# Turning the keys without TensorE, joining four value products to other visits, and padding a bias tile, in a two-layer decoder kernel

## The chip, the core and the metric

The kernel runs on one core of one Trainium2 chip. The time is that of one execution on the device, in microseconds (us). The names of the engines are those of the profile: PE is TensorE (PEld its weight loads), DVE VectorE, ACT ScalarE, POOL GpSimd, SP the engine that only issues transfers.

## The reference, cut to what matters

Input x has 256 rows of 2048 numbers. Layer 1 is a Mamba-2 mixer, layer 2 a sliding-window attention mixer with shared keys and values; each ends in x <- LayerNorm(alpha * x + mixer(x)). All is float32.

```python
# layer 1, in short
z, xbc, dt_raw = split(x @ w_in)                       # 2048 -> 4096 + 6144 + 64
xbc = silu(causal_conv4(xbc));  dt = softplus(dt_raw + dt_bias)
y = ssd(xs, dt, -exp(a_log), B, C) + xs * d_skip       # chunks of 128, decays exp(cumsum(dt * a))
h = groupnorm(y * silu(z)) @ w_out
# before layer 2, once: 4 key heads and 4 value heads of 64
k, v = split(x @ kv_w + kv_b);  k = rope(k)            # first 16 of each 64 are turned
# layer 2: 32 query heads, window 128, one sink per head
q = rope(x @ wq + q_bias);  s = q k^T / 8 within the window
p = exp(s - m) / (sum exp(s - m) + exp(sink - m))
h = ((p v) * silu(x @ wg)) @ wb
```

## The kernel before

Every large product is made of three TensorE products, because each float32 operand is split in two parts: `wh` (rounded by ScalarE, line 164) and `wl` (the rest, by VectorE, line 167) for weights, `xH`/`xL`, `x1H`/`x1L`, `yH`/`yL`, `oH`/`oL` for the other operand. The products h*h, l*h and h*l are taken. A unit of weights is 128 x 2048 numbers; it lands as two halves in `wr` (6 buffers) and stands split in one of 4 buffers of `wh` and 4 of `wl`. A unit's two splits are written up to three units ahead of its products.

There are two shapes of large product. In the first (line 252, `mac`) the weights stand in the array and 256 columns of `xH`/`xL` or `x1H`/`x1L` move; a unit is 48 matmuls. It makes the input projections of both layers. In the second (lines 323 to 325, `out_unit`; line 1011, `x_stat`, for keys and values) the other operand stands in the array, `yH`/`yL`, `oH`/`oL` or `x1H`/`x1L`, and 512 columns of weights move; a unit is 12 matmuls for each half of the rows (h = 0 or 1). "OUT run" below is one such set of 12.

Everything else on TensorE is plain float32 and small, and is done in visits between two units: transposes against the identity, the scores (lines 1160 and 1167), the value products (line 1270 for h = 0; 1284 and 1291 for h = 1).

Layer 2 has four head groups j. The list `B_ORDER` fixes the order q0 g0 q1 g1 q2 o0 g2 q3 o1 g3 o2 o3, where q is a query block and g a gate block (4 units of the first shape each) and o an output block (4 weight units of the second shape, two OUT runs each). After each unit of q and g, and each weight unit of o, `tick()` counts down the list `pending`; `later(n, fn)` puts a piece of work n ticks ahead. So `later(3, ktr)` sets the transposes of the keys, `later(PV_AT[j][h], pv)` the value products, `MOVE_AT` the ScalarE copies that lay the probabilities out for them. `attend(j, 1)` comes three ticks after `attend(j, 0)`.

The keys leave the projection as rows (`kd`, 128 rows by 4 heads by 64, line 1060). GpSimd copies each head a second time beside itself (1066), TensorE turns four 128 x 128 pieces for each half of the rows (1071), and ScalarE copies them out of PSUM into `kT` (1074), where each head stands twice: on partitions 0 to 63 and on 64 to 127.

In layer 1, `sum_decay` (550) makes the exponents of the decays of four heads from `rb`, which a transfer brings back from memory, and `exp_decay` (557) exponentiates them. `plan` holds work that follows a block, `beside` work that is put inside `conv_silu` between its convolution and its tanh (line 497). ScalarE's instructions of `sum_decay` keep their order against all other pinned ones, so what stands behind them waits for them.

The tiles of layer 2 lie in the pool `bp` in the order in which their names are first used. `snk`, `rot`, `kT`, `vt`, the four `qT` and `kvb` share a start at multiples of 256 bytes; `qb` (line 1040) takes 64 bytes, and what follows it lies 64 bytes past a multiple of 256 in each partition:

| tile | start address before | past a multiple of 256 | after | past a multiple of 256 |
|---|---|---|---|---|
| oH, two buffers | 161600, 165696 | 64 | 161792, 165888 | 0 |
| oL, two buffers | 169792, 173888 | 64 | 169984, 174080 | 0 |
| pt0, ptw, pte (probabilities) | 119104, 123200, 157504 | 64 | 127488, 131584, 157696 | 0 |
| qT of odd j, two buffers | 127296, 129344 | 64 | 135680, 137728 | 0 |
| yH, yL, x1H, x1L, kT, vt, wh, wl | 106496, 114688, 179712, 196096, ... | 0 | the same | 0 |

(Addresses are those of the two built programs. All slices of oH, oL, yH, yL, x1H and x1L that stand in the array start at multiples of 512 bytes within their tile.)

Of the kernel before, what the change touches and what calls it, by code (L numbers as in the profile page):

```python
# [8 lines left out]
F32 = mybir.dt.float32  # L9
# [5 lines left out]
ALU = mybir.AluOpType  # L15
AX = mybir.AxisListType

P = 128
S = 256
# [42 lines left out]

MOVE_AT = [[2, 3, 3, 4], [3, 4, 5, 6]]
MOVE_LAST = [2, 3, 3, 4]
PV_AT = [[6, 7], [6, 7], [8, 7], [7, 5]]
RES_AT = [2, 2, 3, 3, 4, 5, 5, 6]
ALPHA = (2.0 * 2) ** 0.25
NEG = -1.0e30
# [15 lines left out]
def trunk(ctx: ExitStack, tc: tile.TileContext, A: dict, out: bass.AP, dbg=None):  # L84
    nc = tc.nc
    PSUM = bass.MemoryType.PSUM

    def pool(name, bufs=1, side=None, space=None, stack=ctx):
        kw = {"space": space} if space is not None else {}
        return stack.enter_context(  # L90
            tc.tile_pool(name=name, bufs=bufs, side=side, reuse_waits="tile", **kw)
        )
# [9 lines left out]
    def nm(s):  # L102
        uid[0] += 1
        return f"{s}_{uid[0]}"

    def mm_tile():
        return mm_ps.tile([P, 512], F32, tag="mm", name=nm("mm"), bufs=4)

    def ax_tile():
        return ax_ps.tile([P, 512], F32, tag="ax", name=nm("ax"), bufs=4)  # L110

    cc = cst.tile([P, 1024], F32, tag="cc", name="cc")
    ident = cc[:, 0:128]
# [131 lines left out]
    def next_unit(behind=False):  # L245
        load_next(min(used[0] + 1 + AHEAD, len(srcs)) - len(units), behind, not behind)
        used[0] += 1
        return units[used[0] - 1]
# [9 lines left out]
    def later(n, fn, place=None):  # L258
        pending.insert(len(pending) if place is None else place, [n, fn])
# [562 lines left out]
    beside = {}  # L822
# [6 lines left out]
    def at(t, fn, *a):  # L829
        plan.setdefault(t, []).append((fn, *a))  # L830
# [5 lines left out]
    for g in range(NG):  # L836
        t = 10 * g
        if g == 0:
            at(TD, turn_dt, *dts)
            at(4, load_decay, 0, 1)  # L840
            at(8, load_low, 0)
            pos = dict(cb=CB0, y=13)

            between[11] = [(turn_first, 0)]
            halves = [(5, 6, 7), (7, 8, 9)]
            by = (9, 10)
        elif g == 1:
            at(10, load_decay, 1, 0)
            at(10, load_decay, 1, 1)
            at(15, load_low, 1)  # L850
            pos = dict(cb=6, y=Y_AT, norm=10 + CB_AT)

            halves = [(13, 14, 15), (15, 16, 16)]
            by = (16, 17)
        else:
            at(t - 5, load_decay, g, 0)
            at(t - 5, load_decay, g, 1)
            at(t, load_low, g)
            pos = dict(cb=CB_AT, y=Y_AT, norm=10 + CB_AT)
        for hf in range(2):  # L860
            if g < 2:
                sa, sb, ex = halves[hf]
                if (g, hf) != (1, 0):
                    at(sa, sum_decay, g, hf, 0, 2)
                at(sb, sum_decay, g, hf, 2, 4)
                at(ex, exp_decay, g, hf)
            else:
                for i in range(2):
                    beside[t + 3 * hf + i] = sum_decay, g, hf, 2 * i, 2 * i + 2
                beside[t + 3 * hf + 2] = exp_decay, g, hf  # L870
        if g == 1:
            at(16, norm, 0)
        at(t + pos["cb"], cb, g)
        for hf in range(2):
            at(by[hf] if g < 2 else t + pos["cb"] + hf, by_cb, g, hf)
        if g > 0:
            xs_at = t + 6
            if g == 1:
                between[17] = [(turn_xs, 1)]
            else:  # L880
                at(xs_at, turn_xs, g)
            for n, js in enumerate(((0, 1), (2, 3))):
                at(xs_at + n + (g == 1), carry_xs, g, js)
            at(xs_at + 2, scale_xs, g)
        at(t + pos["y"], ymm, g)
        if g == 0:
            at(t + pos["y"], sum_decay, 1, 0, 0, 2)
        for i in range(4):
            at(t + pos["y"], gate, g, i)
        if g > 0:  # L890
            at(t + pos["norm"], norm, g)
# [36 lines left out]
    def center(h, mv, rs, nmr):  # L928

        for c in range(4):  # L930
            v = xr[:, h, c * 512 : (c + 1) * 512]
            if c % 2:
                nc.scalar.activation(v, v, AF.Identity, scale=rs[:], bias=nmr[:])
            else:
                nc.vector.tensor_scalar(v, v, mv[:, 0:1], rs[:], ALU.subtract, ALU.mult)
# [44 lines left out]
    bp = pool("bp")  # L980
# [8 lines left out]
    def rope(v, h, n):  # L989

        c = cs[:, h : h + 1, :].to_broadcast([P, n, 8])
        s = sn[:, h : h + 1, :].to_broadcast([P, n, 8])
        t = bp.tile([P, 4, 8, 8], F32, tag="rt", name=nm("rt"), bufs=1)
        x1, x2 = v[:, :, 0:8], v[:, :, 8:16]
        a, b, d, e = [t[:, i, :n, :] for i in range(4)]
        nc.vector.tensor_tensor(a, x1, c, ALU.mult)
        nc.vector.tensor_tensor(b, x2, s, ALU.mult)
        nc.vector.tensor_tensor(d, x2, c, ALU.mult)
        nc.vector.tensor_tensor(e, x1, s, ALU.mult)
        nc.vector.tensor_tensor(x1, a, b, ALU.subtract)  # L1000
        tc.keep_in_program_order(nc.vector.tensor_tensor(x2, d, e, ALU.add))

    def x_stat(ps, h, u, ui, pin=False, last=None):

        todo = [(k, i) for k in range(4) for i in range(3) if i != last]
        todo += [(k, last) for k in range(4) if last]
        for k, i in todo:
            kk = ui * 4 + k
            ks = slice(k * 512, (k + 1) * 512)
            hs = slice(h * P, (h + 1) * P)  # L1010
            m = nc.tensor.matmul(  # L1011
                ps[:], (x1H, x1L, x1H)[i][:, kk, hs], (u.h, u.h, u.l)[i][:, ks],
                start=(kk, i) == (0, 0), stop=ui == 3 and (k, i) == todo[-1],
            )
            pinned(m, pin)
# [20 lines left out]
    kT = bp.tile([P, 4, S], F32, tag="kT", name="kT")  # L1036
    vt = bp.tile([P, 2, S], F32, tag="vt", name="vt")
    kvb = bp.tile([P, 512], F32, tag="qT", name="kvb", bufs=2)
    nc.gpsimd.dma_start(kvb[:], A["kvb"].partition_broadcast(P))
    qb = bp.tile([P, 16], F32, tag="qb", name="qb")  # L1040
    nc.gpsimd.dma_start(qb[:], A["qb"])
    kv_u = []
    for h in range(2):
        ps = mm_tile()
        for ui in range(4):
            if h == 0:

                kv_u.append(next_unit(ui == 1))
                if ui == 0:
                    center(1, *scale1)  # L1050
            x_stat(ps, h, kv_u[ui], ui, h == 0, ((1, 1, 2, None), (1, None, None, None))[h][ui])
            if h == 0:
                for c in ((), (), (0, 1, 2, 3), ())[ui]:
                    if c % 2 == 0:
                        wide = bp.tile([P, 1024], F32, tag=("pt0", "pri")[c // 2], name=nm("x1"), bufs=1)
                    turn_x1(1, c, wide[:, c % 2 * 512 : c % 2 * 512 + 512])
                if ui == 3:
                    load_affine(0)
        kd = bp.tile([P, 4, 2, 64], F32, tag="qt", name=nm("kd"), bufs=2)
        nc.vector.tensor_tensor(  # L1060
            kd[:, :, 0, :], ps[:, :256].rearrange("p (j d) -> p j d", j=4),
            kvb[:, :256].rearrange("p (j d) -> p j d", j=4), ALU.add,
        )
        nc.vector.tensor_tensor(vt[:, h, :], ps[:, 256:], kvb[:, 256:], ALU.add)
        rope(kd[:, :, 0, :], h, 4)
        nc.gpsimd.tensor_copy(kd[:, :, 1, :], kd[:, :, 0, :])

        def ktr(h=h, kd=kd):
            pt = ax_tile()
            for j in range(4):  # L1070
                nc.tensor.transpose(
                    pt[:, j * P : (j + 1) * P], kd[:, j, :, :].rearrange("p a d -> p (a d)"), ident
                )
            nc.scalar.copy(kT[:, :, h * P : (h + 1) * P], pt[:].rearrange("p (j t) -> p j t", j=4))

        later(3, ktr)
    for c in range(1, 4):
        load_affine(c)
    for i, n in enumerate(RES_AT):
# [1 line left out]

    def rope_maps():

        nc.gpsimd.tensor_scalar(qb[:], qb[:], 0.125, None, ALU.mult)
        z = bp.tile([P, 2, 2, 32], F32, tag="rt", name="z", bufs=1)
        nc.vector.transpose(z[:].rearrange("p h m t -> p (h m t)"), turned[:].rearrange("p h m t -> p (h m t)"))
        for k in range(2):
            lo = 64 * k
            for a in range(4):
                nc.scalar.copy(  # L1090
                    rot[lo : lo + 32].rearrange("p m (h a t) -> p a m h t", h=2, a=4)[:, a],
                    z[32 * a : 32 * a + 32].rearrange("p h m t -> p m h t"),
                )
# [5 lines left out]
    sg = {}  # L1099
# [40 lines left out]
    def attend(j, h):  # L1140
# [161 lines left out]
        turn_far()  # L1302
        later(PV_AT[j][h], pv)
        if h == 0:
# [202 lines left out]
```

## Time and profile before

| what | us |
|---|---|
| three runs: median, lowest, highest | 982.09, 980.04, 982.14 |
| the profiled execution's own time | 980.68 |
| its span, first to last instruction | 978.6 |
| PE busy | 972.5 |
| DVE busy, ACT busy, POOL busy | 789.4, 666.5, 103.2 |

The span is 2.1 us shorter than the time of the same execution, which has a start and an end around it. The mean granted TensorE clock was 0.999 of full speed. A matmul's end is modelled, so how fast TensorE goes is read from the distance between two starts. Layer 1 fills the span up to about 657 us, the keys and values come to about 680, layer 2 to the end.

### The profile page before, as it was taken

How to read it: one execution, taken by the hardware profiler on the slowest of the kernel's cores; microseconds unless marked ns; L12 is line 12 of the kernel's file. 1: busy time of each engine (PE TensorE's matmuls, PEld its weight loads, DVE VectorE, ACT ScalarE, POOL GpSimd, SP SyncE). 2: the span in 40 equal slices, each digit the busy share in tenths (PEclk: the TensorE clock that was granted, in tenths of full speed). 3: DMA queues.
4: the chain of work that ended last, by engine and by line, in shares of the span. 5: the costliest groups of instructions: out<-in, count | busy, mean ns of one | idle time of the engine just before them, and what ended most of it. 6: DMA issues, size and time to landing. Idle time of an engine off the chain costs nothing.

```text
span 978.6 us, 18818 instructions
## 1 busy us (share of the span) xinstructions
PE 972.5 (99%) x7364; PEld 896.7 (92%) x7364; DVE 789.4 (81%) x1202; ACT 666.5 (68%) x1254; POOL 103.2 (11%) x145
## 2 busy tenths in 40 slices
PE   9999999999999999999999999999999999999997
PEld 8999989999999998999999999888999988988976
DVE  7888898976888877885887787889977778778786
ACT  7585885864985865776576487467567776784762
POOL 0000303004003001200300300412000000000003
PEclk9999999999999999999999999999999999999999
DMA  9788567755665766666666566458654645465632
GB/s 357 251 284 326 160 210 235 249 201 152 207 218 190 250 208 199 212 200 206 191 205 201 171 211 198 148 187 272 200 159 144 195 153 191 141 208 170 218 127 87
DMA packets 61274, 197.91 MB, mean 202 GB/s; under 512 B 6801, under 2 KB 11329, under 8 KB 60929
## 3 DMA queue, kind: packets, MB, share of 16 engines
q1 hardware_dynamic: 58528, 188.53, 58.5%
q0 software_dynamic: 2048, 7.65, 2.5%
q8 instruction: 58, 0.95, 0.4%
q10 hardware_dynamic: 608, 0.52, 0.2%
q14 instruction: 32, 0.25, 0.1%
HBM read 194.45 MB, written 2.23 MB: 201 GB/s over the span
## 4 chain that ended last, share of the span: by engine, by line
PE 90%; DVE 5%; ACT 2%; issue 1%; DMA 1%; DVEq 0%; ACTq 0%
PE mm L252 56%; PE mm L323 9%; PE mm L324 9%; PE mm L325 9%; PE mm L1011 2%; PE ax L654 2%; DVE wl L167 1%; ACT e L550 1%; DVE cv L494 1%; DMA rb<-rscr 1%; PE ax L1167 1%; DMA wr<-in_wa 1%; ACT wh L164 1%; PE ax L1160 0%; PE mm L390 0%
## 5 line engine op out<-in xcount | busy, mean ns | idle before, releaser
L167 DVE TENSOR_TENSOR wl<-wr,wh 128x1024 fp32r<-128x1024 f32 (+2 forms) x354 | 394.2, 1133 | 80.1 <-ACT wh L164 76.9
L164 ACT ACTIVATE wh<-wr 128x1024 fp32r<-128x1024 f32 (+2 forms) x354 | 333.3, 974 | 104.6 <-PE mm L252 65.9
L252 PE MATMUL mm<-xH,wh 128*128 128x256 f32 x1280 | 354.7, 277 | 0.1
L252 PE MATMUL mm<-xH,wl 128*128 128x256 f32 x1280 | 353.9, 276 | 0.0
L252 PE MATMUL mm<-xL,wh 128*128 128x256 f32 x1280 | 353.9, 276 | 0.0
L252 PEld LDWEIGHTS mm<-xH,wh 128*128 128x128 f32 x1280 | 240.4, 188 | 2.3 <-issue 0.9
L252 PEld LDWEIGHTS mm<-xL,wh 128*128 128x128 f32 x1280 | 240.4, 188 | 1.0
L252 PEld LDWEIGHTS mm<-xH,wl 128*128 128x128 f32 x1280 | 240.3, 188 | 0.0
L252 PE MATMUL mm<-x1H,wh 128*128 128x256 f32 x512 | 143.0, 279 | 0.0
L252 PE MATMUL mm<-x1L,wh 128*128 128x256 f32 x512 | 141.8, 277 | 0.0
L252 PE MATMUL mm<-x1H,wl 128*128 128x256 f32 x512 | 141.7, 277 | 0.0
L323 PE MATMUL mm<-wh,yH 128*128 128x512 f32 x256 | 101.3, 396 | 0.1
L324 PE MATMUL mm<-wh,yL 128*128 128x512 f32 x256 | 99.8, 390 | 0.0
L325 PE MATMUL mm<-wl,yH 128*128 128x512 f32 x256 | 99.7, 389 | 0.0
L252 PEld LDWEIGHTS mm<-x1H,wh 128*128 128x128 f32 x512 | 96.1, 188 | 3.9 <-issue 2.4
L252 PEld LDWEIGHTS mm<-x1L,wh 128*128 128x128 f32 x512 | 96.4, 188 | 0.1
L252 PEld LDWEIGHTS mm<-x1H,wl 128*128 128x128 f32 x512 | 96.2, 188 | 0.0
L670 POOL TENSOR_TENSOR yz<-yz,z 128x256 f32<-128x256 f32 x32 | 26.8, 848 | 451.9 <-DVE yz L665 451.9
L494 DVE SCALAR_TENSOR_TENSOR cv<-mm,pc,cv 128x255 f32<-128x255 f32 x144 | 68.7, 478 | 5.2 <-ACT cv L492 2.6
L323 PEld LDWEIGHTS mm<-wh,yH 128*128 128x128 f32 x256 | 48.1, 188 | 10.6 <-DVE z L584 1.1
L325 PEld LDWEIGHTS mm<-wl,yH 128*128 128x128 f32 x256 | 48.1, 188 | 10.1
L324 PEld LDWEIGHTS mm<-wh,yL 128*128 128x128 f32 x256 | 48.1, 188 | 9.1
(235 smaller groups left out, 1246.6 us busy)
## 6 DMA issues: line engine op xcount, KB each, us to landing
wr<-in_wa SPq DMA_DIRECT2D x154, 512.0 KB, 5.2
wr<-in_wo SPq DMA_DIRECT2D x64, 512.0 KB, 4.6
wr<-in_wq SPq DMA_DIRECT2D x32, 512.0 KB, 4.5
wr<-in_wg SPq DMA_DIRECT2D x31, 512.0 KB, 4.5
wr<-in_wb SPq DMA_DIRECT2D x16, 512.0 KB, 4.7
wr<-in_wb SPq DMA_DIRECT2D x32, 256.0 KB, 3.7
rb<-rscr SPq DMA_DIRECT2D x11, 512.0 KB, 6.0
wr<-in_wkv SPq DMA_DIRECT2D x8, 512.0 KB, 5.6
```

What stands on the lines that cost most here:

```text
L164: m = nc.scalar.activation(h[:, sl], v, AF.Copy)
L167: m = nc.vector.tensor_tensor(l[:, sl], v, h[:, sl].bitcast(F32), ALU.subtract)
L252: m = nc.tensor.matmul(ps, a, b, start=first and i == 0, stop=last and i == 2)
L323: pinned(nc.tensor.matmul(ps, aH[:, k, hs], u.h[:, ks], start=k == 0 and add is None, stop=False), pin)
L324: pinned(nc.tensor.matmul(ps, aL[:, k, hs], u.h[:, ks], start=False, stop=False), pin)
L325: pinned(nc.tensor.matmul(ps, aH[:, k, hs], u.l[:, ks], start=False, stop=k == 3), pin)
L494: nc.vector.scalar_tensor_tensor(a[:, sft:], ps[:, : S - sft], w(3 - sft), a[:, sft:], ALU.mult, ALU.add)
L550: m = nc.scalar.activation(e[:, h, cols], rb[:, h, c * P :], AF.Relu, scale=-1.0, bias=rtk[:, c, h0 + h : h0 + h + 1])
L654: nc.tensor.matmul(ps[64 * r : 64 * r + 64, cols], st.xd[:, c, i, 64 * r : 64 * r + 64], e[:, 256:] if c else e[:, :256], start=c == 0, st ...
L670: nc.gpsimd.tensor_tensor(v, v, st.z[i][:], ALU.mult)
L1011: m = nc.tensor.matmul(ps[:], (x1H, x1L, x1H)[i][:, kk, hs], (u.h, u.h, u.l)[i][:, ks], start=(kk, i) == (0, 0), stop=ui == 3 and (k, i) = ...
L1167: nc.tensor.matmul(pss[par][qs, at : at + 192], q2(rows, b + i, 64 * part, 64), kT[rows, j, 64 * part : 64 * part + 192], start=True, stop ...
```

## The change

Four things are changed.

The keys: `kd` is now 128 x 8 x 64 of which four heads are used, GpSimd's second copy and TensorE's transposes are gone. VectorE turns the 128 x 256 numbers of `kd` in 32 x 32 blocks into a new tile `zk`, once for each half of the rows, and 32 ScalarE copies carry the blocks to their place in `kT`, both copies of a head included. The copies run in four sets of eight, 3, 4, 7 and 8 ticks on. `zk` borrows one of the two buffers of the gate tile `sg`, which so gets its place in the pool earlier.

The value products of h = 0 (`pv`, first column of `PV_AT`) come 2 ticks later for j = 0, 1, 2 and one tick later for j = 3. The bias tile `qb` is padded to 256 bytes. The first half of `sum_decay(0, 0)` moves from behind block 5 into the convolution of block 6.

```diff
-PV_AT = [[6, 7], [6, 7], [8, 7], [7, 5]]
+PV_AT = [[8, 7], [8, 7], [10, 7], [8, 5]]
...
-                if (g, hf) != (1, 0):
+                if (g, hf) == (0, 0):
+                    beside[3] = sum_decay, 0, 0, 0, 2
+                elif (g, hf) != (1, 0):
                     at(sa, sum_decay, g, hf, 0, 2)
...
-    qb = bp.tile([P, 16], F32, tag="qb", name="qb")
-    nc.gpsimd.dma_start(qb[:], A["qb"])
+    qb = bp.tile([P, 64], F32, tag="qb", name="qb")[:, :16]
+    nc.gpsimd.dma_start(qb, A["qb"])
+    zk = bp.tile([P, 4, S], F32, tag="sg", name="zk", bufs=2)[:, :2].rearrange("p h (f t) -> p h f t", t=32)
...
-        kd = bp.tile([P, 4, 2, 64], F32, tag="qt", name=nm("kd"), bufs=2)
+        kd = bp.tile([P, 8, 64], F32, tag="qt", name=nm("kd"), bufs=2)[:, :4]
...
-        rope(kd[:, :, 0, :], h, 4)
-        nc.gpsimd.tensor_copy(kd[:, :, 1, :], kd[:, :, 0, :])
-
-        def ktr(h=h, kd=kd):
-            pt = ax_tile()
-            for j in range(4):
-                nc.tensor.transpose(
-                    pt[:, j * P : (j + 1) * P], kd[:, j, :, :].rearrange("p a d -> p (a d)"), ident
-                )
-            nc.scalar.copy(kT[:, :, h * P : (h + 1) * P], pt[:].rearrange("p (j t) -> p j t", j=4))
-
-        later(3, ktr)
+        rope(kd, h, 4)
+        nc.vector.transpose(zk[:, h].rearrange("p f t -> p (f t)"), kd.rearrange("p j d -> p (j d)"))
+
+        def carry_k(h, e):
+            for a in range(4):
+                for up in range(2):
+                    lo, at = 64 * up + 32 * e, h * P + 32 * a
+                    tc.keep_in_program_order(nc.scalar.copy(
+                        kT[lo : lo + 32, :, at : at + 32],
+                        zk[32 * a : 32 * a + 32, h].rearrange("p (j e) t -> p e j t", e=2)[:, e],
+                    ))
+
+        for e in range(2):
+            later(3 + e + 4 * h, lambda h=h, e=e: carry_k(h, e))
```

Three places show what moves. The first is ScalarE near 50 us, in layer 1: `e` holds the exponents of `sum_decay`, `ct`, `xs` and `cv` belong to the convolutions, `wh` to the weight splits. Before:

```order
L477 ACTIVATE f_441<-rtk 128x128
L550 ACTIVATE e_727<-rb_509,rtk 128x256
L550 ACTIVATE e_727<-rb_509,rtk 128x128
L550 ACTIVATE e_727<-rb_509,rtk 128x256
L499 ACTIVATE ct_643<-cv_644 128x256
L550 ACTIVATE e_727<-rb_509,rtk 128x128
L164 ACTIVATE wh_732<-wr_736 128x1024
L164 ACTIVATE wh_803<-wr_805 128x1024
L499 ACTIVATE xs_712<-cv_713 128x256
L492 ACTIVATE cv_792<-mm_742,pc 128x256
```

and after:

```order
L477 ACTIVATE f_441<-rtk 128x128
L164 ACTIVATE wh_727<-wr_731 128x1024
L499 ACTIVATE ct_643<-cv_644 128x256
L164 ACTIVATE wh_803<-wr_805 128x1024
L164 ACTIVATE wh_803<-wr_807 128x1024
L499 ACTIVATE xs_712<-cv_713 128x256
L492 ACTIVATE cv_787<-mm_737,pc 128x256
L550 ACTIVATE e_792<-rb_509,rtk 128x256
L550 ACTIVATE e_792<-rb_509,rtk 128x128
L550 ACTIVATE e_792<-rb_509,rtk 128x256
L550 ACTIVATE e_792<-rb_509,rtk 128x128
```

The four instructions that read `rb` now stand behind three weight splits and three steps of convolutions.

The second is ScalarE near 690 us, in the first query block; `qT` are the queries, and the two copies to `kT` of before go with the transposes on TensorE. Before:

```order
L164 ACTIVATE wh_8321<-wr_8323 128x896
L1074 COPY kT<-ax_8233 128x4x128
L1074 COPY kT<-ax_8239 128x4x128
L164 ACTIVATE wh_8321<-wr_8325 128x1024
L164 ACTIVATE wh_8388<-wr_8390 128x128
```

and after, the second of the four sets of eight:

```order
L164 ACTIVATE wh_8248<-wr_8250 128x768
L164 ACTIVATE wh_8248<-wr_8252 128x1024
L1075 COPY kT<-zk 32x4x32 x8
L164 ACTIVATE wh_8326<-wr_8328 128x128
L1121 ACTIVATE qT_8246<-mm_8185,qb 128x256
L164 ACTIVATE wh_8326<-wr_8328 128x896
```

The copies stand between the last split of one unit and the first of the next.

The third is TensorE near 940 us, the value products of j = 3 (`pt0`, `ptw`, `pte` are probabilities, `vt` the values). Before, the products of h = 0 stand 24 matmuls ahead of this piece, on their own between two OUT runs, and here are those of h = 1:

```order
L325 MATMUL mm_11080<-wl_10951,oH_10339 128x512
L1284 MATMUL ax_11095<-ptw,vt 64x256 x2
L1284 MATMUL ax_11096<-ptw,vt 64x256 x2
L1291 MATMUL ax_11095<-pte,vt 64x256
L1291 MATMUL ax_11096<-pte,vt 64x256
```

and after:

```order
L325 MATMUL mm_11092<-wl_10972,oH_10475 128x512
L1275 MATMUL ax_11109<-pt_8560,vt 64x512 x2
L1289 MATMUL ax_11116<-ptw,vt 64x256 x2
L1289 MATMUL ax_11117<-ptw,vt 64x256 x2
L1296 MATMUL ax_11116<-pte,vt 64x256
L1296 MATMUL ax_11117<-pte,vt 64x256
```

The products of h = 0 are now in one visit with those of h = 1. The same holds for j = 2; for j = 0 and j = 1 those of h = 0 join the scores of the next head group, `attend(j + 1, 0)`. All other rows of TensorE keep their order.

More of the change, by code (lines that the diff above doesn't have):

```diff
@@ L1058, in trunk @@
                     load_affine(0)
-        kd = bp.tile([P, 4, 2, 64], F32, tag="qt", name=nm("kd"), bufs=2)
+        kd = bp.tile([P, 8, 64], F32, tag="qt", name=nm("kd"), bufs=2)[:, :4]
         nc.vector.tensor_tensor(
-            kd[:, :, 0, :], ps[:, :256].rearrange("p (j d) -> p j d", j=4),
+            kd, ps[:, :256].rearrange("p (j d) -> p j d", j=4),
             kvb[:, :256].rearrange("p (j d) -> p j d", j=4), ALU.add,
@@ L1082, in rope_maps @@
     def rope_maps():
-        nc.gpsimd.tensor_scalar(qb[:], qb[:], 0.125, None, ALU.mult)
+        nc.gpsimd.tensor_scalar(qb, qb, 0.125, None, ALU.mult)
         z = bp.tile([P, 2, 2, 32], F32, tag="rt", name="z", bufs=1)
```

## The prediction

> **What bounds the kernel now.** I read the table of busy times first, then the waits of TensorE, then stretches of TensorE's timeline around each place that the change touches, and last the rows of ScalarE and VectorE at those places.
>
> ```profile
> PE 972.5 (99%) x7364; PEld 896.7 (92%) x7364; DVE 789.4 (81%) x1202; ACT 666.5 (68%) x1254; POOL 103.2 (11%) x145
> ```
>
> TensorE is busy for 972.5 of 978.6 us of span, and the view of its waits has a single entry, 1.0 us at the very start. So time is won only by fewer matmuls, by matmuls that follow each other faster, or by closing small seams between groups. What the other engines gain or lose counts only if TensorE comes to wait for it. Since the end of a matmul is modelled, I take its pace from the distance between two starts.
>
> ```profile
> 696.07 0.28 PE L252 MATMUL mm<-x1H,wl 128*128 128x256 f32 x1
> 696.18 1.04 PE L1071 MATMUL ax<-cc,kd 128*128 128x128 f32 x8
> 696.97 0.36 PE L252 MATMUL mm<-x1H,wh 128*128 128x256 f32 x1
> 697.17 0.28 PE L252 MATMUL mm<-x1L,wh 128*128 128x256 f32 x1
> ```
>
> ```profile
> 804.50 0.40 PE L325 MATMUL mm<-wl,oH 128*128 128x512 f32 x1
> 804.83 1.08 PE L1270 MATMUL ax<-pt,vt 128*64 128x512 f32 x4
> 805.83 0.50 PE L323 MATMUL mm<-wh,oH 128*128 128x512 f32 x1
> 806.17 0.39 PE L324 MATMUL mm<-wh,oL 128*128 128x512 f32 x1
> ```
>
> These are, on TensorE's timeline, two visits of small float32 matmuls: the eight key transposes, and the value products of j = 0, h = 0. Steady starts are 0.11 us apart at line 252 and 0.23 in an OUT run; around a visit one gap ahead and one behind are longer.
>
> **Key transposes taken off TensorE.** From 696.18 to 696.97 they hold it 0.79 us. The first matmul behind them takes 0.20 to the next start instead of 0.11. Removing both gives 0.79 + 0.09 = 0.88 us.
>
> **Four visits merged into others.** The products stay, their seams go. Entry: 804.50 to 804.83 is 0.33 instead of 0.23. Exit: 805.83 to 806.17 is 0.34 instead of 0.23. So a seam costs 0.10 + 0.10, and four of them 0.80 us. The merged products are all float32 like the visit that they join, so I add nothing for the joint.
>
> **The padded tile.** It moves `oH` and `oL` from 64 bytes past a multiple of 256 to a multiple. They are the operand that stands in the array in an OUT run. Here are 24 matmuls of such runs, first with `yH`, which lies on a multiple, then with `oH`:
>
> ```profile
> 640.91 0.39 PE L323 MATMUL mm<-wh,yH 128*128 128x512 f32 x1
> ...
> 646.35 0.39 PE L323 MATMUL mm<-wh,yH 128*128 128x512 f32 x1
> ```
>
> ```profile
> 808.73 0.40 PE L323 MATMUL mm<-wh,oH 128*128 128x512 f32 x1
> ...
> 814.33 0.40 PE L323 MATMUL mm<-wh,oH 128*128 128x512 f32 x1
> ```
>
> With `yH` 24 starts take 5.44 us, 226.7 ns each; with `oH` 5.60, 233.3 each. The shapes and types are the same; the runs of line 1011, whose `x1H` lies on a multiple too, go like `yH`. Lines 323 to 325 have 124 matmuls of 512 columns each on `oH` or `oL`: 372 x 6.7 ns = 2.5 us, and 24 of 256 columns at some 4 ns 0.1. If the address makes the difference, 2.6 us go; if not, nothing. No row shows `oH` at another address, but the runs differ in nothing else that I can find, so I take the whole 2.6 and keep 0 as the other end.
>
> The Trainium skill, "TensorE: Matmul & The Clock Gate", in the part "Step-by-step: what each phase is for", says that the array has two read ports of its own and that loading the next tile's weights takes no bandwidth from the running matmul. By that the place of the standing operand could not change the pace and this term would be 0; the 226.7 and 233.3 speak against it, though they can't say which property of `oH` does it.
>
> The probabilities `pt0`, `ptw`, `pte` and the `qT` of odd j move likewise, but their matmuls are plain float32, and the scores of odd and even j show no difference of pace. Nothing for these. There is one slow unit that I can't explain, just behind a value visit:
>
> ```profile
> 780.61 0.39 PE L252 MATMUL mm<-x1H,wh 128*128 128x256 f32 x1
> ...
> 786.25 0.28 PE L252 MATMUL mm<-x1H,wl 128*128 128x256 f32 x1
> ```
>
> 47 gaps take 5.64 us, 120 ns each, where the first rows above have 0.11. Four units, two behind each h = 1 value visit of j = 0 and 1, lose about 0.2 each this way. If the alignment of `pte` and `ptw` cured them, 0.8 would come on top; the merged visits might as well slow more units. I take 0, and price both among the rivals.
>
> **The decay sums.** The view of waits has this for ScalarE, and TensorE's timeline that at the end of the first stretch that hangs on it:
>
> ```profile
> ACT e L550 <- DMA rb<-rscr: 2.6, 1, 2.6
> ```
>
> ```profile
> 129.82 0.28 PE L252 MATMUL mm<-xH,wl 128*128 128x256 f32 x1
> 130.17 0.50 PE L323 MATMUL mm<-wh,yH 128*128 128x512 f32 x1
> ...
> 135.51 0.39 PE L325 MATMUL mm<-wl,yH 128*128 128x512 f32 x1
> 136.02 0.36 PE L252 MATMUL mm<-xH,wh 128*128 128x256 f32 x1
> ```
>
> The chain of work that ended last runs through the return of `rb` at 42 to 49, these sums, and the transfer of weights below, up to the matmul at 130.17.
>
> ```profile
> 52.99 5.06 DMA wr<-in_wa
> ```
>
> After the change three splits and three convolution steps stand ahead of the sums, so the 2.6 us of waiting go to work that was behind it. But TensorE, up to there, waits little: 0.35 instead of 0.11 at 130.17, and 0.51 instead of 0.23 at 136.02, 0.52 in all. The gain lies between 0 (the weight transfer of 5.06 is late next) and 0.52; I take the middle, rounded to 0.3.
>
> **What VectorE, ScalarE and GpSimd get instead.** No row of before has the new copies; the nearest are equal in size, the turned rotation map and the block turns of layer 1:
>
> ```profile
> L625 DVE STREAM_TRANSPOSE zx<-xs 128x256 f32<-128x256 f32 x28 | 12.0, 438 | 0.9
> ...
> L1090 ACT COPY rot<-z 32x128 f32<-32x128 f32 x8 | 2.4, 296 | 1.4 <-DVE z L1086 1.3
> ```
>
> ```profile
> 690.86 0.42 ACT L164 ACTIVATE wh<-wr 128x256 fp32r<-128x256 f32 x1 [2.69 <-issue]
> ...
> 713.51 0.31 ACT L164 ACTIVATE wh<-wr 128x128 fp32r<-128x128 f32 x1 [1.67 <-PE mm L252]
> ```
>
> 32 copies x 0.296 = 9.5 us on ScalarE, in four bursts of 2.4; two turns x 0.438 = 0.9 us on VectorE; GpSimd loses two copies and ScalarE two. I cost it all at nothing, and the cover is this. Each burst falls into the place between two units' splits, where ScalarE idles 1.7 to 3 us (the bracketed 2.69 and 1.67). The tightest is 0.7 over, and a unit's splits stand up to three units, some 16 us, ahead of its matmuls. If that lead were gone, the full 9.5 us would show. Behind a burst wait the query rows (`qT`) and VectorE's `wl` splits, which have the same lead. The keys themselves are needed here:
>
> ```profile
> 718.97 1.16 PE L1160 MATMUL ax<-kT,qT 64*128 64x128 f32 x16
> ...
> 736.64 1.53 PE L1167 MATMUL ax<-kT,qT 64*64 64x192 f32 x32
> ```
>
> The bursts go at ticks 3, 4, 7 and 8; a tick is one unit of 5.5 us, and the old `ktr` at tick 3 stood at 696. So the first half is there by about 704, the second by about 726, a burst included: 15 and 10 us early. `zk` borrows a buffer of `sg`, whose next use is in the first gate block, where the copies already are or soon will be done; a wait there would fall on ScalarE and DVE, with the same lead behind it. No queue of transfers is passed: the change issues the same transfers, `qb` from GpSimd's queue included.
>
> **The later value products.** For j = 0, 1, 2 they still lie well ahead of their output block. For j = 3 this is not so: products, gate, `oH`, `oL` and the OUT run follow closely.
>
> ```profile
> 941.39 0.50 PE L323 MATMUL mm<-wh,oH 128*128 128x512 f32 x1
> ```
>
> ```profile
> 945.02 0.75 DVE L1258 TENSOR_TENSOR o<-ax,sg 128x256 f32<-128x256 f32 x2
> ...
> 946.82 0.69 DVE L1299 TENSOR_TENSOR oL<-o,oH 128x512 fp32r<-128x512 f32 x1
> ```
>
> Here h = 1 of before takes from the end of the visit at 941.39 to 947.51 until `oL` is there, 6.1 us. After the change h = 0 comes out of that same visit, and its first OUT run is 24 matmuls, some 5.5 us, behind it. At VectorE's old pace that would be 0.6 late; but h = 0 is first in VectorE's and ScalarE's new order and need not stand behind the `xr` adds that took part of the 6.1. I take 0 and keep up to 2.5 as a rival.
>
> **Sum.** 0.88 + 0.80 + 2.6 + 0.3 = 4.58, say 4.6 us. The profiled execution's own time is 980.68, so 976.1; it stands 1.4 under the median of 982.09, from which the same sum gives 977.5. I take the middle of the two, a base of 981.4, and so **976.8**.
>
> **The rivals.** All go from the base of 981.4.
>
> The pad does nothing: the slow pace belongs to `oH` for another cause. Then 2.0 is left, 979.4. For it: no row shows one tile at two addresses. Against it: three aligned operands go at one pace, the unaligned one at another.
>
> The four slow units turn fast as well: 4.6 + 0.8 = 5.4, 976.0. For it: `pte` and `ptw` are the operands of just those visits. Against it: the units behind them don't read these tiles.
>
> `oH` of j = 3 comes late and TensorE waits 2.5: 979.3. It decides when products to `oL` take over 5.5 us; the 6.1 above speaks for it, the order on VectorE against it.
>
> More units fall into the slow pace behind the merged visits: up to 12 x 0.2 = 2.4 back, 979.2.
>
> Slower: ScalarE's copies are not hidden. Place: from 690 to 730. All of 9.5 less 4.6, 4.9 slower, **986.3**. It decides when a burst exceeds ScalarE's idle time and the splits have no lead, or when a copy that moves between partitions takes several times 0.296. For it: ScalarE is 68% busy and its idle slots are no longer than a burst. Against it: the lead of three units. The Trainium skill, "VectorE: DVE Perf Modes", in "The three transpose paths", has it that VectorE turns 32 x 32 blocks only, and that 128 x 128 goes through TensorE where PSUM will do as the target; it speaks for the way of before, and no run so far shows what the blocks cost here.
>
> **How the numbers follow.** Chances: the sum as it stands 0.52, with the four units 0.14, pad without effect 0.16, `oH` late 0.06, more slow units 0.05, copies not hidden 0.07. About 0.2%, 1.96 us, can be told from no change, so faster means under 980.1. The first two cases are faster; the three around 979.3 lie 0.8 from the bound, and with runs that scatter by 2 us half of each, 0.13, counts as faster, the rest as the same. That makes 0.79 faster. The last case gives 0.07 slower, and 0.14 is left for the same. Low end: all terms at their best (0.52 for the sums, 0.8 for the units, the pad's 2.6), 5.6 off the lowest run of 980.04, 974.4. High end: the pad without effect from the median, 980.1, and some scatter, 980.5. Only the copies not hidden and a few ends of the others lie outside, under 2 in 10.
>
> **What the profile after would show.** No line 1071, and the unit at about 696 following its neighbour without a seam. OUT runs on `oH` at 227 ns; 233 would be the failure of the largest term. One visit fewer at four places. The wait of ScalarE for `rb` gone. 32 rows of copies near 0.3 us, no wait of TensorE for `wh`, `wl` or `kT` between 690 and 740, and none for `oH` or `oL` near 946. I would be wrong above all by the cause of the 233 ns, next by a copy far above 0.3 us.

## The result and the profile after

| | before | after |
|---|---|---|
| median of 10 runs, us | 981.47 (979.32 to 983.62) | 977.32 (976.65 to 979.88) |
| profiled execution, own time and span | 980.68, 978.6 | 977.57, 975.7 |

The ratio is 0.9964, 95% interval 0.9955 to 0.9972: 3.5 us faster, 2.7 to 4.4. The forecast was 976.8. The page of the changed kernel and the view of TensorE's waits:

```profile
PE 969.3 (99%) x7356; PEld 896.6 (92%) x7356; DVE 788.8 (81%) x1204; ACT 675.0 (69%) x1284; POOL 100.4 (10%) x143
```

```profile
PE ax L372 <- DVE zero L360: 1.0, 1, 1.0
PE mm L323 <- DVE xr L330: 0.6, 1, 0.6
PE mm L324 <- DVE oL L1304: 0.3, 1, 0.3
```

The two lower waits are new. Where the transposes stood, TensorE's timeline now runs through at its steady 0.11:

```profile
696.09 0.28 PE L252 MATMUL mm<-x1H,wl 128*128 128x256 f32 x1
696.20 0.28 PE L252 MATMUL mm<-x1H,wh 128*128 128x256 f32 x1
```

Two rows of the OUT runs, 24 matmuls apart, 5.44 us, 226.7 ns each:

```profile
950.56 0.39 PE L323 MATMUL mm<-wh,oH 128*128 128x512 f32 x1
...
956.00 0.39 PE L323 MATMUL mm<-wh,oH 128*128 128x512 f32 x1
```

The new groups cost what their neighbours in size did, and a burst fills the place in front of a unit's first split on ScalarE:

```profile
L1075 ACT COPY kT<-zk 32x128 f32<-32x128 f32 x32 | 9.5, 296 | 0.4
...
L1069 DVE STREAM_TRANSPOSE zk<-kd 128x256 f32<-128x256 f32 x2 | 0.9, 435 | 0.0
```

```profile
710.90 2.44 ACT L1075 COPY kT<-zk 32x128 f32<-32x128 f32 x8
713.36 0.31 ACT L164 ACTIVATE wh<-wr 128x128 fp32r<-128x128 f32 x1
```

The new wait near 809 stands in TensorE's timeline between two OUT runs, and the row of VectorE behind it is an add on `xr`, which frees the accumulator that the run wants:

```profile
808.74 0.39 PE L325 MATMUL mm<-wl,oH 128*128 128x512 f32 x1
809.74 0.50 PE L323 MATMUL mm<-wh,oH 128*128 128x512 f32 x1 [0.61 <-DVE xr L330]
```

```profile
809.01 0.67 DVE L330 SCALAR_TENSOR_TENSOR xr<-xr,mm 128x512 f32<-128x512 f32 x1
```

That the add ends at 809.68 and the matmul starts at 809.74 shows the tie. Before, the same add ended at 809.57 and the run that needs its accumulator started 1.96 later:

```profile
808.90 0.67 DVE L330 SCALAR_TENSOR_TENSOR xr<-xr,mm 128x512 f32<-128x512 f32 x1
```

```profile
811.53 0.40 PE L323 MATMUL mm<-wh,oH 128*128 128x512 f32 x1
```

The one near 945 is for `oL` of j = 3, h = 0:

```profile
944.53 0.39 PE L323 MATMUL mm<-wh,oH 128*128 128x512 f32 x1
945.21 0.50 PE L324 MATMUL mm<-wh,oL 128*128 128x512 f32 x1 [0.29 <-DVE oL L1304]
```

```profile
944.48 0.68 DVE L1304 TENSOR_TENSOR oL<-o,oH 128x512 fp32r<-128x512 f32 x1
```

Cutting the executions at fixed matmuls tells more than one total. Each number is the distance between two starts on TensorE, the last the span less the start of the last matmul. "After, again" is a second profiled execution of the changed kernel (below).

| stretch, us | before | after | after, again |
|---|---|---|---|
| first steady unit starts at | 23.59 | 24.44 | 23.79 |
| from there to the unit at about 150 | 126.38 | 125.60 | 125.60 |
| from there to the end of keys and values (680) | 529.85 | 529.80 | 531.41 |
| layer 2: from there to the last matmul | 293.34 | 290.83 | 290.86 |
| the end, behind the last matmul | 5.42 | 5.00 | 5.00 |

Layer 2 repeats within 0.03 us, layer 1 varies by more than a microsecond between executions of one program. So layer 2 is where parts of the change can be weighed from one trace, and its 2.51 splits like this (the term of the OUT runs is the one that the pad alone shows, below; the others are sums over the runs and visits in the two traces): transposes and their seam 0.87 less; 31 OUT runs on `oH` 2.12 less; the slow unit of line 252 at 838 turned normal, 0.18 less; joined visits about 1.2 less; against these three waits, 0.94 near 809, 0.59 near 945, and 0.31 in the visit of the scores at 836, which took 1.77 instead of 1.46.

### The profile page after: what moved, and what is told of

The parts are those of the page before. It is cut to its first block, busy times and chain, and to the rows that moved or that the text cites. A ratio compares the mean times of both kernels' runs of the same rounds, so it can differ in the third digit from the quotient of the medians.

```text
span 975.7 us, 18826 instructions
## 1 busy us (share of the span) xinstructions
PE 969.3 (99%) x7356; PEld 896.6 (92%) x7356; DVE 788.8 (81%) x1204; ACT 675.0 (69%) x1284; POOL 100.4 (10%) x143
## 4 chain that ended last, share of the span: by engine, by line
PE 93%; DVE 3%; ACT 2%; issue 1%; DVEq 0%; ACTq 0%
PE mm L252 61%; PE mm L323 8%; PE mm L324 8%; PE mm L325 8%; PE ax L654 2%; PE mm L1013 2%; DVE wl L167 1%; ACT wh L164 1%; PE ax L1172 0%; PE ax L1165 0%; PE ax L591 0%; PE mm L390 0%; ACT p L1200 0%; ACT ptw L1233 0%; DVE z L1214 0%
```

## The experiments

**The pad alone.**

```diff
-    qb = bp.tile([P, 16], F32, tag="qb", name="qb")
+    qb = bp.tile([P, 64], F32, tag="qb", name="qb")[:, :16]
```

> The kernel before with the bias tile padded to 256 bytes and nothing else; the order of instructions is that of before. If the address of the standing operand makes the pace: starts in the OUT runs on oH and oL go from 233 to 227 ns, 31 runs x 0.08 = 2.4 us less, so about 979.1 where before has 981.5. If that pace belongs to oH for another cause, or the gain in the changed kernel came from the merged visits: 233 ns stay and the time is the same within 0.5 us. The slow units of line 252 behind the value visits at 780 and 831 should stay slow (118 to 120 ns), since pte and ptw at a multiple of 256 did not cure them in the changed kernel; if they go, alignment plays a part there after all.

Measured: 980.25 beside 981.04, ratio 0.9989 (0.9977 to 1.0001). The pace changed as the address has it; 24 matmuls take 5.44 us:

```profile
951.39 0.39 PE L323 MATMUL mm<-wh,oH 128*128 128x512 f32 x1
...
956.83 0.39 PE L323 MATMUL mm<-wh,oH 128*128 128x512 f32 x1
```

The 31 full runs went from 87.93 to 85.81 us. Of these 2.12, layer 2 kept 1.58 (291.75): the visit of the scores at 837 grew by 0.49, and the unit at 697 went at the slow pace, 0.20. So the address sets the pace of these runs, and a part of the gain is taken back by other waits. In the whole time 2.4 less was expected, and the interval allows anything from 2.3 less to nothing: the trace shows the gain, the median alone does not.

**The opposite sign, and the moving operand.** `yH` and `yL` moved to 64 past a multiple of 256; in another kernel `x1H` and `x1L` to 192 past (their pool is laid from the right-hand end, so 64 bytes more for `x1L` move both down).

```diff
-                yp.tile([P, 4, S], F32R, tag="yH", name=nm("yH"), bufs=2),
+                yp.tile([P, 4 * S + 64], F32R, tag="yH", name=nm("yH"), bufs=2)[:, 16 : 16 + 4 * S].rearrange("p (k s) -> p k s", s=S),
...
-    x1L = x1s.tile([P, KT, S], F32R, tag="x1L", name="x1L")
+    x1L = x1s.tile([P, KT * S + 16], F32R, tag="x1L", name="x1L")[:, : KT * S].rearrange("p (k s) -> p k s", s=S)
```

> The kernel before with yH and yL of layer 1 put 64 bytes past a multiple of 256, where oH and oL lie; the order of instructions is that of before. This is the opposite sign of the pad on twice as many runs. If the address of the standing operand makes the pace: the 64 OUT runs of layer 1 go from 2.72 to 2.80 us, 64 x 0.08 = 5.1 us more, about 986.6. If it is anything else about oH: no change, 981.5 within 0.7.

> The kernel before with x1H and x1L put 192 bytes past a multiple of 256 (64 short of the next); the order of instructions is that of before. The two stand in the array in the 96 matmuls of line 1011, and move through it in 1536 matmuls of line 252. If only the standing operand's address counts: line 1011 goes from 227 to 233 ns, 96 x 6.7 ns = 0.6 us more, 982.1, and line 252 stays at 114 ns. If the moving operand's address counts as well, by the same 3% of its pace: 1536 x 3.4 ns = 5.2 us on top, about 987. If neither: 981.5.

Measured: 984.67 (ratio 1.0039, 1.0025 to 1.0052, so 3.8 us more) and 988.55 (1.0078, 1.0064 to 1.0091, 7.7 more). Of `yH`, 24 matmuls took 5.60 us:

```profile
641.46 0.39 PE L323 MATMUL mm<-wh,yH 128*128 128x512 f32 x1
...
647.06 0.39 PE L323 MATMUL mm<-wh,yH 128*128 128x512 f32 x1
```

From 150 us on 56 runs of layer 1 went from 154.02 to 157.80, 0.07 each where 0.08 was expected. With `x1H` moved, one steady unit of line 252 (48 matmuls, both rows being the first of a unit) takes 5.69 us, where before has 5.45:

```profile
748.58 0.28 PE L252 MATMUL mm<-x1H,wh 128*128 128x256 f32 x1
...
754.27 0.28 PE L252 MATMUL mm<-x1H,wh 128*128 128x256 f32 x1
```

```profile
743.66 0.28 PE L252 MATMUL mm<-x1H,wh 128*128 128x256 f32 x1
...
749.11 0.28 PE L252 MATMUL mm<-x1H,wh 128*128 128x256 f32 x1
```

Layer 2 grew by 7.03. Line 1011, where `x1H` stands in the array, grew only by 0.22 in 96 matmuls, 2.3 ns each, not the 6.7 that I had expected. So the address of the moving operand counts as well, by 4.6 ns per matmul where I had reckoned with 3.4.

**Other offsets: 96 and 128 bytes past a multiple of 256.** The same edit as the pad, with 24 and 32 columns.

> The kernel before with the bias tile at 96 bytes, which puts oH and oL 96 bytes past a multiple of 256. A slice of 128 columns is 512 bytes in a partition. If what counts is a multiple of 256 or of 128: starts in OUT runs stay at 233 ns. If a multiple of 32 were enough, 64 past would have been fast as well, so 227 is not expected from any theory; a pace above 233 would say that it depends on more than aligned or not.

> The kernel before with the bias tile at 128 bytes, which puts oH and oL 128 bytes past a multiple of 256; with 96 past, the OUT runs went at 233 ns as with 64. If a multiple of 128 is enough: 227 ns. If it takes a multiple of 256: 233 ns.

Measured in one execution each, 981.65 and 983.11, so that only the pace can be read. 24 matmuls take 5.62 us with 96, and 5.57 with 128:

```profile
950.65 0.40 PE L323 MATMUL mm<-wh,oH 128*128 128x512 f32 x1
...
956.27 0.39 PE L323 MATMUL mm<-wh,oH 128*128 128x512 f32 x1
```

```profile
949.09 0.39 PE L323 MATMUL mm<-wh,oH 128*128 128x512 f32 x1
...
954.66 0.40 PE L323 MATMUL mm<-wh,oH 128*128 128x512 f32 x1
```

A multiple of 128 is not enough for `oH` and `oL`; of the offsets tried (0, 64, 96, 128) only 0 is fast in these runs of 512 columns.

It does not follow that the operand in the array must start at a multiple of 256. In line 252 of layer 2 this operand is `wh` and `wl`, whose slices the source places by hand (`BROKEN`): of the 16 slices of a unit the first starts 0 bytes into `wh` and 7872 into `wl`, 192 past a multiple of 256, and the fifteen others start at 576 and 64 bytes, 64 past. The moving `x1H` and `x1L` lie at a multiple. A steady unit of before, its first, third and last matmul:

```profile
743.66 0.28 PE L252 MATMUL mm<-x1H,wh 128*128 128x256 f32 x1
...
743.90 0.28 PE L252 MATMUL mm<-x1H,wl 128*128 128x256 f32 x1
...
749.00 0.28 PE L252 MATMUL mm<-x1H,wl 128*128 128x256 f32 x1
```

The first two gaps, at the slice with 0 and 192, take 0.24 us, 120 ns each; the 45 others take 5.10, 113.3 each. So 64 past is the fast place here. The unit at 707.96, in which the source lays the second slice at 0 and 192 too (`BROKEN2`), has the two gaps of 120 ns at its second slice as well, before and after. And the 24 matmuls of 256 columns on `oH` and `oL` did not gain by the pad: 11 gaps take 1.30 us before and 1.31 to 1.32 after. What sets the pace is therefore not the place of one operand alone; the place of the other and the number of columns come in. The rule behind it stays open.

**The keys, the value products and the decay sums, each alone** on the kernel before (the diff of the change, its part).

> The kernel before with only the keys turned by VectorE and carried by 32 ScalarE copies; no pad, value products and decay sums as before. If the copies are hidden: TensorE's visit of 0.79 and its seam of 0.08 go, 0.87 us, about 980.6 where before has 981.5. If they are not hidden, up to 9.5 us come on top, so anything above 982.

> The kernel before with only the value products of h = 0 put later. Theory: four seams go, 0.8 us; but without the visit at 805 TensorE catches up with VectorE's adds on xr and waits there about 0.8 to 1.0, as in the changed kernel near 809, and for oL of j = 3 about 0.5 to 0.7 near 945. The OUT runs on oH are at 233 ns here, 0.08 slower each, which gives VectorE up to 0.3 us back before 809. So between 0.3 less and 0.6 more than before, 981.2 to 982.1: the joining alone wins nothing. Rival: the two waits come from the faster OUT runs of the pad; then they are not there, and 980.5.

> The kernel before with only the first half of sum_decay(0, 0) moved. By the comparison of the two traces TensorE loses its stalls near 130 and 136: 0.8 us less, 980.7. If the weight transfer were late next, as the prediction allowed: nothing, 981.5.

| kernel | median, us | ratio, interval | layer 2, us | end, us |
|---|---|---|---|---|
| keys | 979.95 | 0.9982 (0.9973 to 0.9991) | 292.42 | 5.00 |
| value products | 981.02 | 0.9990 (0.9980 to 1.0000) | 292.59 | 5.85 |
| decay sums | 981.86 | 0.9999 (0.9988 to 1.0010) | 293.34 | 5.79 |
| pad (above) | 980.25 | 0.9989 (0.9977 to 1.0001) | 291.75 | 5.86 |

The kernel before, run beside the first three, had a median of 982.05. In layer 2 (293.34 before) the keys win 0.92, the value products 0.75, the pad 1.58, together 3.25; the whole change has 2.51. What is missing is put down to waits that only the faster TensorE meets: 1.84 us of them in the whole change, more than in any part alone. The keys won more in the medians than the 0.87 that was expected: 1.8, with an interval from 0.9 up, and their end is 0.42 shorter than that of before. The value products alone met the wait for `xr` already (0.2 in the view of waits), at the old pace of the OUT runs, but not the one for `oL`, which was expected too.

The decay sums win nothing that can be measured, though they do what was expected of them near 130:

```profile
130.35 0.28 PE L252 MATMUL mm<-xH,wl 128*128 128x256 f32 x1
130.46 0.39 PE L323 MATMUL mm<-wh,yH 128*128 128x512 f32 x1
```

0.11 where before has 0.35. From the first steady unit to 150 the six profiled executions with moved sums all take 125.60. Of the eight without, two with `yH` or `x1H` moved left aside, 125.60 twice, and 126.38, 126.65, 127.10 and 128.24. But in four of the six the gain is given back at 261 to 270, where TensorE waits for a convolution step; the first execution of the changed kernel and that of the decay sums alone show no such wait. In the second execution of the changed kernel:

```profile
269.60 0.28 PE L252 MATMUL mm<-xH,wl 128*128 128x256 f32 x1
270.52 0.36 PE L252 MATMUL mm<-xH,wh 128*128 128x256 f32 x1 [0.64 <-DVE cv L494]
```

The mean time at which the fourth visit of line 654 starts (302 to 305 us) is 303.2 for the six with moved sums and 303.0 for the six without. What makes VectorE late at 270 stays open.

**Two bursts instead of four.**

```diff
-            later(3 + e + 4 * h, lambda h=h, e=e: carry_k(h, e))
+            later(4 + 4 * h, lambda h=h, e=e: carry_k(h, e))
```

> The changed kernel with the four sets of eight copies made into two sets of sixteen, at ticks 4 and 8: ScalarE is taken for 4.7 us in one piece, more than the 1.7 to 3 us that it idles between two units' splits. If the lead of the splits (up to three units, 16 us) is the cover: no change from the changed kernel, 977.3 within 0.5, and no wait of TensorE for wh or wl. If the cover is only the idle time: 2 x (4.7 - 3) = 3.4 us more, about 980.7.

Measured: 979.38, ratio 0.9980 (0.9971 to 0.9989), and layer 2 at 292.51, 1.68 more than the changed kernel. Neither theory has it. Between 690 and 740 each unit and visit takes the same as in the changed kernel within 0.01. But ScalarE does not recover. The first row is a burst on its timeline, the second `oH` of j = 0; in the changed kernel (third row) the same `oH` stands 3.02 earlier, of which TensorE's own offset at that time explains 1.38:

```profile
694.63 4.91 ACT L1075 COPY kT<-zk 32x128 f32<-32x128 f32 x16
...
772.89 0.63 ACT L1303 ACTIVATE oH<-o 128x512 fp32r<-128x512 f32 x1 [0.22 <-DVE o L1263]
```

```profile
769.87 0.63 ACT L1303 ACTIVATE oH<-o 128x512 fp32r<-128x512 f32 x1 [0.21 <-DVE o L1263]
```

Apart from the bursts, ScalarE's and VectorE's orders are the same in both. The 1.6 us are carried along for 90 us, until the scores at 787 wait for an accumulator that `o` still holds:

```profile
786.76 0.88 PE L1172 MATMUL ax<-kT,qT 64*64 64x192 f32 x16
788.56 1.21 PE L1172 MATMUL ax<-kT,qT 64*64 64x192 f32 x16 [0.92 <-DVE o L1263]
```

So the lead of the splits hides a burst from the next units, and does not pay for it.

**The changed kernel again, and with value products put back.**

```diff
-PV_AT = [[8, 7], [8, 7], [10, 7], [8, 5]]
+PV_AT = [[8, 7], [6, 7], [10, 7], [8, 5]]
...
+PV_AT = [[8, 7], [6, 7], [10, 7], [7, 5]]
```

> The changed kernel once more, beside the next two on the same chip. If its two new waits belong to the order of its instructions: TensorE again waits for xr near 809 (0.6 by the view of waits) and for oL near 945 (0.3), and the time is 977.3 where before has 981.5. If they were chance in one execution: they are absent or elsewhere.

> The changed kernel with the value products of j = 1, h = 0 back at 6 ticks, so that they stand on their own between two OUT runs near 804 again. If the joined visit took away the pause in which VectorE caught up with its adds on xr: the wait near 809 goes, 1.0 us with its seams, and one seam of 0.2 returns, 0.8 us less than the changed kernel, 976.5. If VectorE is late there for another reason: the wait stays and the kernel is 0.2 slower, 977.5.

> As the one above, and the products of j = 3, h = 0 back at 7 ticks. The wait for oL near 945 cost 0.6 to 0.7 us with its seam; a joined visit is worth 0.35 there. If that wait comes from the later products, another 0.3 us less, 976.2; if it comes from the faster OUT runs, it stays and the kernel is 0.35 slower than the one above. So no more than 0.3 either way: this is the best version that I can see from the two traces.

Measured beside one kernel before at 981.48: 977.59 (0.9956, 0.9942 to 0.9970), 978.48 (0.9967, 0.9954 to 0.9980), 979.56 (0.9971, 0.9960 to 0.9982). Layer 2: 290.86, 291.49, 291.31. The two new waits came back in the second execution at the same places, 0.6 and 0.3, so they belong to the program. The last line of the diff is the third kernel. With j = 1 put back the wait for `xr` went, 0.94 us with its seams, and this took its place (view of waits):

```profile
PE ax L1172 <- DVE o L1263: 1.2, 1, 1.2
```

The visit at 836 grew by 1.42. With j = 3 put back as well, `oL` was waited for no more; as the later products alone did not meet this wait either, it takes both them and the faster runs. Neither version beats the changed kernel, though the waits went that were to go, and 976.5 and 976.2 were expected in that case: the waits are shifted from one place to the next, since VectorE's chain of softmax, `o` and `xr` runs hardly earlier when TensorE does (its add on `xr` started at 809.01 after and 808.90 before, while TensorE had won 1.08).

## Why the prediction was right

The time lay in the range, 0.5 from the forecast. The terms were not as near as that; errors of both signs cancelled.

- Key transposes, 0.88 forecast: 0.87 in the trace, 0.92 in layer 2 of the keys alone. Right.
- Four seams, 0.80: about 1.2. The seam was sized rightly to 0.03; I added nothing for the joint, but the products themselves are shorter behind or ahead of other small products (line 1270: 1.01 before, 0.91 for j = 2 and 3). The visit at 804.83 is that of j = 1, not of j = 0 as the prediction has it; its rows and their sum are right.
- The padded tile, 2.6: right that the address makes the difference, and 0.5 too large. I took 6.7 ns for every matmul; the mean over 372 is 5.7 (2.12 / 372), because runs behind a visit start slowly anyhow: 2.90 became 2.86, against 2.80 to 2.72 in the middle. The 0.1 for the 24 matmuls of 256 columns did not come; they went from 118 to 120 ns. And the argument that three operands at a multiple go at one pace and the one beside it at another left out `wh` and `wl` in line 252, which go fast at 64 past: the guess held for these runs, but not as a rule of multiples of 256. The rule of the Trainium skill that I set against this term ("TensorE: Matmul & The Clock Gate", "Step-by-step: what each phase is for", two read ports of the array), as I applied it, is not borne out here: the runs with `oH` and `yH` moved show that the place of the operand in the array changes the pace (226.7 against 233.3 ns), so the measurement decides.
- The decay sums, 0.3: no gain that can be measured. In four of six executions what is won by 150 us is waited for at 270; for the decay sums alone, which show no such wait, the cause stays open.
- The copies at nothing: right for the weight splits, and no wait for `kT`. The Trainium skill's advice for a 128 x 128 transpose ("VectorE: DVE Perf Modes", "Rules for kernel authors"), to go through TensorE, did not pay here, where TensorE is the bound: the keys alone are 0.9982 of the time before. The sentence on the cover was too generous, though: the burst of 4.9 shows that a delay of ScalarE stays.
- "The later value products": I took 0 for `oL` at j = 3 and named a wait up to 2.5. It came, at 0.59. The waits for `xr` near 809, 0.94, and for `o` at 836, 0.31, were in no case of mine. The step that failed is the first one, that only TensorE's own work counts as long as it waits for nothing. The margins that it passed over can be read from the trace before. Behind the add on `xr` near 809 it was 1.96 us; after the change the OUT run that needs the accumulator would start at 808.96, 2.57 earlier, while the add ends 0.11 later than before. At the scores at 837 the margin behind `o` was 0.12: it ends at 837.63, and the matmul that is held up in the other kernels, the 19th of the visit, starts at 837.75. The edits used both up, and with the wait for `oL` 1.84 us of their gain became waits.
- Not in the sum: 0.42 at the end of the kernel, and 0.18 from one slow unit of the four that the rival with 0.8 had named; the other three stayed slow.

In the trace: 0.87 + 1.2 + 2.12 + 0.18 - 1.84 + 0.42 = 2.95, where the spans differ by 2.90. The medians moved by more, 3.5 by the ratio, whose interval holds it. So it is in part luck that the time came within 0.5 of the forecast: the unforeseen waits, the smaller pad and the missing decay sums took 2.6 from the sum of 4.6, the shorter visits, the end and the unit gave back 1.0, and the medians moved by 4.15 where the traces account for 2.9.

## What to carry to other kernels

The place of a float32r operand within 256 bytes was worth 1 to 4% of a matmul's pace here, for the operand in the array and the one that moves; a tile of 64 bytes ahead of large ones cost 2.1 us of TensorE's time, of which layer 2 kept 1.6 when it was padded. Which place is fast depends on the other operand and the shape, so it is to be read from the distance between starts, not from a rule of multiples. Where one engine never waits, ask how far ahead of it the others are before adding up its savings: here it was 0.1 us at one place and 2 us at another, and joining visits and faster runs met the same chain. A delay put on a busy engine is not gone because the next units don't see it.

## What was not expected of the hardware

The moving operand at 192 past a multiple of 256 slows line 252 from 115.5 to 120.1 ns per matmul over layer 2 (177.47 to 184.50 us for 1536), twice as much per matmul as the standing one in line 1011. The weights that stand in the array there lie 64 past a multiple in 15 of 16 slices, in this kernel as in the one before.

The end behind the last matmul is 5.00 us in the six profiled executions with the new keys, and 5.38 to 5.92 in the eight without. In the latter the view of transfers shows a late load of instructions in the last microseconds, in the former none:

```profile
q14 instruction: 2, 0.02, 0.3%
```

This is the row of before for its last 10 us. That the two go together is shown; that the load makes the end longer is not.

The units of line 252 that go at 118 ns and not 114 behind some visits stay without a cause: `pte` and `ptw` at a multiple of 256 left three of the four as they were. The fourth, near 838, was normal in 9 of the 14 profiled executions, and in 8 of these 9 the visit of scores ahead of it was longer than its usual 1.46 us; but a visit of 2.94 at 787, in the kernel with two bursts, left the unit behind it slow.
